# First residual sum by DMAs that add while they write

## The chip, the cores and the metric

The kernel runs on 1 core of one Trainium2 chip. The metric is the device time of one execution in microseconds; three runs of the kernel before took 1112.96, 1113.0 and 1114.12 us, median 1113.0. One further execution was profiled; all rows of views below come from it.

## The reference

One decoder layer on x of 1024 positions by 1024 channels, all in float32:

```python
h = rms_norm(x, ln_pre_mix)
proj = h @ w_in                       # pooling input, q, k, v
mix = concat(pool_out, attn_out) @ w_out
x = x + rms_norm(mix, ln_post_mix)    # the first residual sum
h = rms_norm(x, ln_pre_ffn)
f = (silu(h @ w_gate) * (h @ w_up)) @ w_down
x = x + rms_norm(f, ln_post_ffn)
```

`rms_norm(x, g)` is `x * rsqrt(mean(x*x) + 1e-6) * g`. The change concerns the line of the first residual sum alone.

## The kernel before, in words

Activations stand transposed: channels on the 128 partitions in 8 row tiles (d = 0 to 7), positions along the free axis in two halves of 512 (h = 0, 1). Every matmul is made from float32 operands that are split into a high and a low part (`hi`, `lo`), three passes each, so weights and activations are split by ScalarE (ACT: the copy that rounds to `hi`) and by VectorE or GpSimd (DVE, POOL: the subtraction that leaves `lo`). TensorE (PE) works through one fixed list of matmuls; the other engines serve it.

The stretch of the change, in order of PE's list:

* `out_proj(1, ...)`: the output projection of half 1, one row tile d after the other, 24 matmuls of 512 columns each. Its weights are loaded by SP, split by L302 (ACT) and L306 (DVE). Meanwhile `chain(0, ...)` finishes half 0: row means on PE, the power -0.5 on POOL (L332), the scale spread over partitions by four PE transposes (L261), then `add(d)`.
* `firsts(j, ...)`, j = 0 to 5: gate and up projection of half 0, 48 matmuls each, 12 for each of two banks (n = 0), then 12 more into the same two banks (n = 1). Between the two, `taken(0, i)` copies a bank to SBUF on ACT (L1453, `q<-ps_...`), and the matmuls of n = 1 into that bank can start only when the copy has read it. Meanwhile `chain(1, ...)` finishes half 1, and the block sums T1 to T4 (L1499, L1502, split by L1508 and L1509) are made from the rows of both halves.
* from there on `seven(...)`: the products of the block sums, with raw weights that `fetch` loads (L1583) and `block_sums` combines (L1548 to L1554).

In `add(d)` of the kernel before, z(d) holds the row tile of the mix. L1364 multiplies it by the gain and the scale (DVE, in place, the scale read from PSUM). L1365 adds x to it (DVE). `load` (L1360) has brought x as two transfers of 1 MB for each half, into tiles `xr`. L1369 stores the sum to DRAM from SP's queue. Then come the readers of the row: L1374 and L1375 split it (`parts`, blocks b), L1327 or L1330 square it for the next norm (`whole`), L1383 or L1493 scale it in place, L1499 and L1502 take differences.

Every engine takes its instructions in the order of its own list; an instruction that waits holds up all behind it. SP's list holds nearly all DMA issues, so a store that waits for its row holds up the loads behind it. The order of all lists except PE's comes from a scheduler that runs when the kernel is built, from start positions written in the table `PRM` (`at[...]` in `chain`).

Of the kernel before, what the change touches and what calls it, by code (L numbers as in the profile page):

```python
# [8 lines left out]
F32 = mybir.dt.float32  # L9
F32R = mybir.dt.float32r  # L10
AF = mybir.ActivationFunctionType
ALU = mybir.AluOpType
# [3 lines left out]
P = 128  # L16
# [236 lines left out]
def hybrid_block(ctx: ExitStack, tc: tile.TileContext, xT, w_in, w_v, w_vp, w_pool, w_out, w_gate, w_up, w_down,  # L253
                 g1, g2, g3, g4, pscale, cost, sint, maskA, maskB, maskD, quadA, quadB, lsel, ident, perm, band, out):
    nc = tc.nc
# [85 lines left out]
    def slot(k, shape, dt, name):  # L341

        return xgp.tile(shape, dt, name=name, tag="xk%d" % k)
# [13 lines left out]
    sq = qkp.tile([P, T], F32, name="sq", tag="vT", bufs=1)  # L357
# [176 lines left out]
    def did(key):  # L534
        seen[key] = seen.get(key, 0) + 1

    def need(key, n):
        assert seen.get(key, 0) >= n, (key, n, seen.get(key, 0))
# [724 lines left out]
    def zrows(h):  # L1263
        zs = []

        def z(d):
            if not zs:
                zs.extend(slot(2 * h + i, [P, 4, 512], F32, "z%d%d" % (h, i)) for i in range(2))
            return zs[d // 4][:, d % 4]
        return z  # L1270

    z = zrows(0), zrows(1)
# [10 lines left out]
    late = {}  # L1283
# [67 lines left out]
    def chain(h, sq, s3, at):  # L1351

        sl = slice(h * 512, (h + 1) * 512)
        x = []

        def load():
            for n in range(2):
                x.append(slot((6, 4)[h] + n, [P, 4, 512], F32, "xr%d" % n))
                with tc.issue_after(behind.ins) if h else ExitStack():
                    nc.sync.dma_start(x[n], xT[:, 4 * n:4 * n + 4, sl])  # L1360

        def add(d):
            zd = z[h](d)
            nc.vector.scalar_tensor_tensor(zd, zd, g2s[:, d:d + 1], sq.rb, op0=ALU.mult, op1=ALU.mult)  # L1364
            late["z"] = nc.vector.tensor_tensor(zd, zd, x[d // 4][:, d % 4], ALU.add)  # L1365
            did(("row", h, d))
            if h == 0:
                parts(d)
            nc.sync.dma_start(x1d[d, :, sl], zd)  # L1369

        def parts(d):
            need(("row", h, d), 1)
            zd, (hi, lo) = z[h](d), (t[:, d % 4] for t in block(d // 4, h))
            nc.scalar.activation(hi, zd, AF.Copy, scale=g3s[:, d:d + 1])  # L1374
            nc.vector.scalar_tensor_tensor(lo, zd, g3s[:, d:d + 1], hi.bitcast(F32), op0=ALU.mult, op1=ALU.subtract)  # L1375
            did(("parts", h, d))

        def whole(d):
            need(("row", h, d), 1)
            did(("whole", h, d))  # L1380
            s3.add(d, z[h](d))
            if h == 0:
                nc.scalar.activation(z[h](d), z[h](d), AF.Copy, scale=g3s[:, d:d + 1])  # L1383
                did(("scaled", d))
        return [([load], -1, 0), ([sq.mean], at[0], 0), ([sq.rows], at[1], 0),
                ([lambda d=d: add(d) for d in range(NK)], at[2], at[3]),
                ([lambda d=d: whole(d) for d in range(NK)], at[4], at[5]),
                *([([lambda d=d: parts(d) for d in range(4, NK)], at[8], at[9])] if h else []),
                ([s3.mean], at[6], 0), ([lambda: (s3.rows(r3[:, sl]), did(("r3", h)))], at[7], 0)]
# [17 lines left out]
    def block(kh, h):  # L1407

        if (kh, h) not in B:
            n = {(0, 0): 0, (1, 0): 2, (1, 1): 4}[kh, h]  # L1410
            B[kh, h] = [big(n + i, [P, 4, 512], F32R, "b%d%d" % (kh, h)) for i in range(2)]
        return B[kh, h]

    st, weights = out_proj(1, 3, sqs[1][0].add)
    weights(3)
    *chain0, mean0, rows0 = chain(0, *sqs[0], G["c0"])
    emit((st, 0.0, 1.0), *chain0, mean0)
    behind = loads[-2]
# [239 lines left out]
    def second():  # L1658
        behind_of(behind, ahead[1])
    two, again, fetch, weights = seven(0, ("P6", "P5", "P7", "P4", "P3"), nc.vector if G["fe"][EARLY] else nc.gpsimd)  # L1660
    part = 8 / len(before[0]) / EARLY
    emit(([x for f in before for x in f], 0.0, 1.0), (two[0], 1.0, 1.0 + part), (two[1], 1.0 + part, 1.0 + 2 * part),
         *chain(1, *sqs[1], G["c1"]), rows0,
         ([second], G["c3"][4], 0),
         *(([lambda a=a: behind_of(powers[-1], a)], at, 0) for a, at in zip(ahead[2:], G["ca"])), ([again], G["c3"][3], 0),
# [333 lines left out]
```

## Time and profile before

| | |
|---|---|
| median of 3 runs | 1113.0 us |
| profiled execution | 1112.79 us |
| its span, first to last instruction | 1111.0 us |
| granted TensorE clock | 0.999 |
| DMA, mean rate over the span | 182 GB/s |
| queues that DMAs are issued from | SP (200.00 MB), ACT (0.79 MB), instruction fetch |

In a row of the timeline the columns are: start, duration over all merged instructions, engine, line, operation, output<-inputs, shape, count; in brackets how long the engine sat idle before it and what released it. POOL issues no DMA in the kernel before.

### The profile page before, as it was taken

What the parts mean: (1) busy time and instruction counts of PE and PEld (TensorE: products, weight loads), DVE (VectorE), ACT (ScalarE), POOL (GpSimd) and SP (SyncE); (2) the same over time, 40 slices, a digit from 0 to 9 for tenths busy, and PEclk for the clock granted to TensorE, in tenths of its full rate; (3) what the DMA queues carried; (4) which work ended last, traced back from release to release, by engine and by line L of the source; (5) the groups of instructions that cost most, each with busy time, mean ns of one, the idle gap of its engine ahead of it and who ended that gap; (6) DMA issues with size and microseconds to landing.
All of it is one profiled execution on the core that took longest, in us unless ns stands there. A gap on an engine that the chain in (4) does not pass through costs nothing.

```text
span 1111.0 us, 16122 instructions
## 1 busy us (share of the span) xinstructions
PE 1094.3 (98%) x5694; PEld 932.5 (84%) x5694; DVE 780.3 (70%) x1340; ACT 549.4 (49%) x980; POOL 541.0 (49%) x439
## 2 busy tenths in 40 slices
PE   9999999999999999999999999999999999999997
PEld 7888999898888888888887888888888888888896
DVE  7967878787877667799777777667566462343684
ACT  7456767666677755965322222233222544343442
POOL 0111716272645021201666777686568996666521
PEclk9999999999999999999999999999999999999999
DMA  8225232424149338564466666543445895656442
GB/s 296 94 77 186 96 133 75 154 90 157 66 144 347 132 133 309 215 244 155 159 239 233 241 237 227 208 171 119 156 174 213 282 359 193 205 180 203 133 152 76
DMA packets 91296, 201.82 MB, mean 182 GB/s; under 512 B 9296, under 2 KB 25168, under 8 KB 89808
## 3 DMA queue, kind: packets, MB, share of 16 engines
q1 hardware_dynamic: 90240, 200.00, 50.6%
q8 instruction: 45, 0.74, 0.3%
q10 hardware_dynamic: 976, 0.79, 0.2%
q14 instruction: 35, 0.29, 0.1%
HBM read 143.87 MB, written 56.89 MB: 181 GB/s over the span
## 4 chain that ended last, share of the span: by engine, by line
PE 89%; DVE 4%; ACT 3%; DMA 1%; POOL 1%; issue 1%; ACTq 0%; DVEq 0%; POOLq 0%
PE ps_pj L258 28%; PE ps_s L258 25%; PE ps_o L258 24%; PE ps_t L258 10%; PE ps_t L261 2%; DMA bd<-sq 1%; ACT pp L784 1%; POOL pp L869 1%; DMA wraw<-in_w_in_dram 0%; ACT ptr L920 0%; DVE ptr L921 0%; DVE rsw L495 0%; DVE qh L526 0%; PE ps_o L261 0%; DVE ps_o L965 0%
## 5 line engine op out<-in xcount | busy, mean ns | idle before, releaser
L258 PE MATMUL ps_o<-tT,fw 128*128 128x512 f32 x648 | 150.7, 389 | 0.9 <-DVE sq L1619 0.9
L258 PEld LDWEIGHTS ps_o<-tT,fw 128*128 128x128 f32 x648 | 121.4, 188 | 26.6 <-issue 1.5
L1436 POOL TENSOR_TENSOR fw<-rw,fw 128x512 fp32r<-128x512 f32 x74 | 103.2, 1418 | 68.5 <-ACT fw L1434 67.1
L258 PE MATMUL ps_pj<-x,whl 128*128 128x512 f32 x480 | 132.7, 400 | 0.0
L258 PEld LDWEIGHTS ps_pj<-x,whl 128*128 128x128 f32 x480 | 85.7, 188 | 13.0
L306 POOL TENSOR_TENSOR whl<-wraw,whl 128x512 fp32r<-128x512 f32 x42 | 55.9, 1353 | 71.4 <-ACT whl L302 65.7
L1731 POOL TENSOR_TENSOR op<-rw,op 128x512 fp32r<-128x512 f32 x38 | 62.3, 1639 | 31.5 <-ACT op L1730 31.0
L1436 POOL TENSOR_TENSOR whl<-rw,whl 128x512 fp32r<-128x512 f32 x32 | 51.2, 1620 | 45.3 <-ACT whl L1434 34.1
L258 PE MATMUL ps_s<-b,fw 128*128 128x512 f32 x312 | 72.5, 389 | 0.0
L258 PEld LDWEIGHTS ps_s<-b,fw 128*128 128x128 f32 x312 | 58.6, 188 | 12.2
L921 DVE TENSOR_TENSOR ptr<-ps_t,ptr 128x512 fp32r<-128x512 f32 (+1 forms) x84 | 53.5, 647 | 20.4 <-ACT ptr L920 19.8
L1730 ACT ACTIVATE op<-rw 128x1024 fp32r<-128x1024 f32 x38 | 40.0, 1059 | 55.8 <-PE ps_t L258 26.5
L1434 ACT ACTIVATE fw<-rw 128x1024 fp32r<-128x1024 f32 x45 | 47.5, 1061 | 39.3 <-PE ps_o L258 15.5
L258 PE MATMUL ps_pj<-whl,x 128*128 128x256 f32 (+1 forms) x432 | 64.8, 297 | 0.0
L920 ACT ACTIVATE ptr<-ps_t 128x512 fp32r<-128x512 f32 (+1 forms) x84 | 45.7, 560 | 31.3 <-PE ps_t L261 16.2
L258 PEld LDWEIGHTS ps_pj<-whl,x 128*128 128x128 f32 x432 | 57.5, 190 | 2.4
L869 POOL TENSOR_SCALAR pp<-pp,wv 128x256 f32<-128x256 f32 x61 | 33.0, 564 | 50.9 <-DVE wv L835 49.7
L1732 DVE TENSOR_TENSOR op<-rw,op 128x512 fp32r<-128x512 f32 x33 | 28.6, 865 | 40.9 <-ACT op L1730 34.7
L332 POOL TENSOR_TENSOR nrr<-nrr,half 128x4 f32<-128x4 f32 (+1 forms) x7 | 7.4, 1054 | 96.6 <-ACT eps L331 57.4
L1731 POOL TENSOR_TENSOR fw<-rw,fw 128x512 fp32r<-128x512 f32 x26 | 42.7, 1642 | 22.4 <-ACT fw L1730 20.4
L258 PE MATMUL ps_o<-ptr,v 128*128 128x128 f32 (+3 forms) x376 | 51.1, 269 | 2.4 <-DVE ptr L921 2.3
L784 ACT ACTIVATE pp<-pp,sx 128x256 f32<-128x256 f32 x96 | 47.8, 501 | 9.9 <-DVE sx L781 9.5
(336 smaller groups left out, 2808.2 us busy)
## 6 DMA issues: line engine op xcount, KB each, us to landing
rw<-bd SPq DMA_DIRECT2D x77, 256.0 KB, 4.0
rw<-in_w_gate_dram SPq DMA_DIRECT2D x28, 512.0 KB, 4.7
rw<-in_w_up_dram SPq DMA_DIRECT2D x28, 512.0 KB, 5.7
v<-vd SPq DMA_DIRECT2D x22, 512.0 KB, 4.7
rw<-wsd SPq DMA_DIRECT2D x44, 256.0 KB, 3.8
bd<-p SPq DMA_DIRECT2D x39, 256.0 KB, 2.5
rw<-in_w_down_dram SPq DMA_DIRECT2D x33, 256.0 KB, 3.9
wraw<-in_w_out_dram SPq DMA_DIRECT2D x15, 512.0 KB, 5.1
```

The lines of the kernel that those rows point to most:

```text
L258: return tc.keep_in_program_order(nc.tensor.matmul(*a, **k))
L261: return tc.keep_in_program_order(nc.tensor.transpose(dst, src, by))
L306: pin(eng.tensor_tensor(dst[:, 1, at:at + w], src[:, at:at + w], dst[:, 0, at:at + w].bitcast(F32), ALU.subtract))
L784: nc.scalar.activation(pt[:, j, lo:], pt[:, j, lo:], AF.Exp, bias=sx[:, 0, side, j, hd, 0:1], scale=-1.0, accum_out=sx[:, 0, side, j, hd, ...
L869: nc.gpsimd.tensor_scalar(pv, pv, un.wv[:, side, j, hd:hd + 1], 1.0, op0=ALU.mult, op1=ALU.mult)
L920: nc.scalar.activation(ptr[:, 0, :w], t[:, :w], AF.Copy)
L921: nc.vector.tensor_tensor(ptr[:, 1, :w], t[:, :w], ptr[:, 0, :w].bitcast(F32), ALU.subtract)
L1434: nc.scalar.activation(dst[:, :, 0], src, AF.Copy)
L1436: low[0] = eng.tensor_tensor(dst[:, i, 1], src[:, i], dst[:, i, 0].bitcast(F32), ALU.subtract)
L1730: nc.scalar.activation(w[:, :, 0], raw, AF.Copy)
L1731: nc.gpsimd.tensor_tensor(w[:, 0, 1], raw[:, 0], w[:, 0, 0].bitcast(F32), ALU.subtract)
L1732: (nc.gpsimd if p == "P1" else nc.vector).tensor_tensor(w[:, 1, 1], raw[:, 1], w[:, 1, 0].bitcast(F32), ALU.subtract)
```

## The change

The loads of x into `xr` and the 16 additions on DVE go. In their place, behind each scaling, POOL issues a DMA that reads the same 256 KB of x from DRAM and adds them to z(d) in SBUF. `late["z"]`, behind which `fetch` is placed, is now the last such DMA.

```diff
     def chain(h, sq, s3, at):
 
         sl = slice(h * 512, (h + 1) * 512)
-        x = []
-
-        def load():
-            for n in range(2):
-                x.append(slot((6, 4)[h] + n, [P, 4, 512], F32, "xr%d" % n))
-                with tc.issue_after(behind.ins) if h else ExitStack():
-                    nc.sync.dma_start(x[n], xT[:, 4 * n:4 * n + 4, sl])
-
         def add(d):
             zd = z[h](d)
             nc.vector.scalar_tensor_tensor(zd, zd, g2s[:, d:d + 1], sq.rb, op0=ALU.mult, op1=ALU.mult)
-            late["z"] = nc.vector.tensor_tensor(zd, zd, x[d // 4][:, d % 4], ALU.add)
+            late["z"] = nc.gpsimd.dma_start(zd, xT[:, d, sl], accum_op=ALU.add)
             did(("row", h, d))
             if h == 0:
                 parts(d)
...
-        return [([load], -1, 0), ([sq.mean], at[0], 0), ([sq.rows], at[1], 0),
+        return [([sq.mean], at[0], 0), ([sq.rows], at[1], 0),
```

PE's list is the same in both kernels. Those of the other engines differ from the first scaled row to the start of the products of the block sums, some 100 us on in the trace before. In the changed kernel all lines behind 1353 have numbers lower by 8: L1364 becomes L1356, the DMA that adds is L1357, L1374 becomes L1366, L1453 becomes L1445. Three places follow.

POOL, from the last weight split ahead of the first norm of the mix to the splits of the first gate and up weights (nrr: the row scales; rw: raw gate and up weights; whl, fw: their split tiles). Before:

```order
L306 TENSOR_TENSOR whl<-wraw,whl 128x512 x4
L332 TENSOR_TENSOR nrr<-nrr,half 128x4 x2
L1436 TENSOR_TENSOR whl<-rw,whl 128x512 x2
L332 TENSOR_TENSOR nrr<-nrr,half 128x4
L1436 TENSOR_TENSOR fw<-rw,fw 128x512 x4
L332 TENSOR_TENSOR nrr<-nrr,half 128x4
```

Now:

```order
L306 TENSOR_TENSOR whl<-wraw,whl 128x512 x4
L332 TENSOR_TENSOR nrr<-nrr,half 128x4
L1357 DMA z_4187<-in_xT_dram 128x512 x4
L1357 DMA z_4188<-in_xT_dram 128x512 x4
L332 TENSOR_TENSOR nrr<-nrr,half 128x4
L1428 TENSOR_TENSOR whl<-rw,whl 128x512 x2
L332 TENSOR_TENSOR nrr<-nrr,half 128x4
L1428 TENSOR_TENSOR fw<-rw,fw 128x512 x2
L1357 DMA z_4833<-in_xT_dram 128x512 x4
L1357 DMA z_4834<-in_xT_dram 128x512 x4
L1428 TENSOR_TENSOR fw<-rw,fw 128x512 x2
```

Eight DMAs stand between the first and the second L332, and eight between two pairs of weight splits; nothing else on POOL has moved.

ACT in the output projection of half 1, up to the split of the weights of its row tile 6 (z_4187 and z_4188: rows 0 to 3 and 4 to 7 of half 0). Now:

```order
L1366 ACTIVATE b_4869<-z_4188,g3s 128x512
L1252 ACTIVATE z_4833<-ps_s 128x512
L1366 ACTIVATE b_4869<-z_4188,g3s 128x512
L1330 ACTIVATE p<-z_4187 128x512
L1375 ACTIVATE z_4187<-z_4187,g3s 128x512
L1330 ACTIVATE p<-ps_s 128x512
L1375 ACTIVATE z_4187<-z_4187,g3s 128x512
L1252 ACTIVATE z_4834<-ps_pj 128x512
L302 ACTIVATE whl<-wraw 128x1024
```

Before, between the last L1374 and the same L302:

```order
L1374 ACTIVATE b_4873<-z_4188,g3s 128x512 x4
L1252 ACTIVATE z_4837<-ps_s 128x512
L1383 ACTIVATE z_4187<-z_4187,g3s 128x512 x2
L1330 ACTIVATE p<-ps_pj 128x512
L1330 ACTIVATE p<-z_4187 128x512
L1252 ACTIVATE z_4838<-ps_pj 128x512
L302 ACTIVATE whl<-wraw 128x1024
```

The readers of the rows are spread out among the copies; between the split of row 7 and this L302 stand five instructions now and six before.

ACT in the gate and up products, from the copies of j = 1 (`q<-ps_t`) to the first copy of j = 2 (`q<-ps_s`). Before:

```order
L1453 ACTIVATE q<-ps_t 128x512
L1374 ACTIVATE b_5431<-z_4838,g3s 128x512 x4
L1330 ACTIVATE p<-z_4837 128x512
L1493 ACTIVATE z_4837<-z_4837,g3s 128x512
L1508 ACTIVATE tT_5409<-z_4187 128x512 x2
L1493 ACTIVATE z_4837<-z_4837,g3s 128x512
L1508 ACTIVATE tT_5409<-z_4187 128x512 x2
L1453 ACTIVATE q<-ps_s 128x512
```

Now (ahead of these rows, behind the copy `q<-ps_t`, stand two L1500 and one L1330):

```order
L1500 ACTIVATE tT_5401<-z_4187 128x512
L1366 ACTIVATE b_5423<-z_4834,g3s 128x512
L1500 ACTIVATE tT_5401<-z_4187 128x512
L1485 ACTIVATE z_4833<-z_4833,g3s 128x512
L1426 ACTIVATE whl<-rw 128x2x512
L1366 ACTIVATE b_5423<-z_4834,g3s 128x512
L1450 ACTIVATE p<-p 128x512
L1485 ACTIVATE z_4833<-z_4833,g3s 128x512
L1500 ACTIVATE tT_5340<-whl 128x512
L1330 ACTIVATE p<-z_4833 128x512
L1366 ACTIVATE b_5423<-z_4834,g3s 128x512
L1445 ACTIVATE q<-ps_s 128x512
```

Between the two copies stood 11 instructions; now there are 14, among them a weight split (L1426, L1434 before) and an activation (L1450, L1458 before) that stood behind the copy. On DVE, the instructions behind the eighth scaling of half 1 are now L1452, L1540, L1491, L1541, three L1491, L1501, L1542 and L1449 (before: L1460, L1548, L1499, L1549, L1499, L1509, L1550, L1457); before, the additions, L1499 and the splits L1375 stood there, and L1549 and L1550 came later.

## The prediction

> **What bounds the kernel now.** First the head of the page, then the windows of the stretch in which the lists differ, then PE's waits.
>
> ```profile
> span 1111.0 us, 16122 instructions
> PE 1094.3 (98%) x5694; PEld 932.5 (84%) x5694; DVE 780.3 (70%) x1340; ACT 549.4 (49%) x980; POOL 541.0 (49%) x439
> ```
>
> ```profile
> 416.60:472.20 55.60, 55.60 (x263) 46.21 (x262) 41.99 (x57) 40.71 (x65) 10.34 (x8) 1.00 0.69 263
> 472.20:527.70 55.50, 55.50 (x248) 46.00 (x247) 52.88 (x79) 32.14 (x51) 5.34 (x4) 1.00 0.53 199
> ```
>
> ```profile
> PE ps_s L258 <- DVE ex L812: 2.7, 2, 1.5
> ...
> PE ps_pj L261 <- POOL nrr L332: 1.0, 1, 1.0
> PE ps_o L258 <- DVE sq L1619: 0.9, 1, 0.9
> ```
>
> The windows (columns: length; busy time of PE, PEld, DVE, ACT, POOL; clock; DMA share; GB/s) show PE busy in every microsecond of 416.6 to 527.7, at full clock. PE's list isn't touched. So nothing can be won in the stretch of the change; the only waits behind it that it might touch are 1.0 and 0.9 us. The change can only be free, or make PE wait. The question is which instruction that PE needs comes late.
>
> **The change part by part. What goes, and costs nothing.** The additions leave DVE, the loads of 4 MB leave SP.
>
> ```profile
> L1365 DVE TENSOR_TENSOR z<-z,xr x16: 681/684/689, 432.6 to 482.9; 128x512 f32<-128x512 f32 x16
> ```
>
> 16 x 0.684 = 10.9 us of DVE, but PE never waited behind them: gain 0. The same 4 MB of x are read again by the new DMAs.
>
> **What is added on POOL.** Sixteen DMA issues stand in its list, in two places where it was idle:
>
> ```profile
> 424.29 1.03 POOL L332 TENSOR_TENSOR nrr<-nrr,half 128x4 f32<-128x4 f32 x1 [2.45 <-ACT nrr L327]
> 463.10 1.46 POOL L332 TENSOR_TENSOR nrr<-nrr,half 128x4 f32<-128x4 f32 x1 [37.78 <-ACT eps L331]
> 512.88 3.16 POOL L1436 TENSOR_TENSOR fw<-rw,fw 128x512 fp32r<-128x512 f32 x2 [38.50 <-ACT fw L1434]
> ```
>
> Behind the issues of half 0 waits L332 at 463.1, behind those of half 1 the split at 512.9. The first can be issued when the first row is scaled, at 427.36 + 0.74 = 428.1. That leaves 35 us for eight: up to 4.4 us each are hidden as far as POOL is concerned. Cost 0; above that it would be 8 us for each further microsecond.
>
> **When a row is ready.** Before, the last row of half 0 was ready at 432.63 + 4.90 = 437.5. Now row d is ready when its DMA has landed. Call l the time from the end of the first scaling to the first landing, and p the spacing of the landings. No transfer of this kind is in the trace; the nearest:
>
> ```profile
> 427.36 5.36 DVE L1364 SCALAR_TENSOR_TENSOR z<-z,g2s,ps_o 128x512 f32<-128x512 f32 x8 [3.84 <-PE ps_o L261]
> 432.63 4.90 DVE L1365 TENSOR_TENSOR z<-z,xr 128x512 f32<-128x512 f32 x8
> ...
> xr<-in_xT_dram SPq DMA_DIRECT2D x4, 1024.0 KB, 8.1
> xraw<-in_xT_dram SPq DMA_DIRECT2D x4, 256.0 KB, 4.2
> ```
>
> The same tensor in 256 KB lands 4.2 us after its issue, in 1 MB after 8.1, so (8.1 - 4.2) / 3 = 1.3 us for each further 256 KB. An addition must also fetch the old row: between 1.3 us (that hides) and 2.6 (it counts in full). So p is an estimate between 1.3 and 2.6, and I take 2.0, the middle, since the transfers of half 0 share the engines with eight row stores and the weight loads. For l: 4.2 with nothing added; 4.2 + 1.3 for the old row, and 1.0 more (the 1.03 us of POOL's L332, its shortest work here) for an issue by an engine that has issued none so far: 6.5. I take 5.2, the middle.
>
> **Half 0: the weights of row tile 6.** ACT's list puts the split of row 7 five instructions ahead of L302, which makes the `hi` weights that PE needs at 450.54; L306 makes `lo` from it.
>
> ```profile
> 438.70 0.40 SPq L298 DMA_DIRECT2D wraw<-in_w_out_dram  x1
> 439.65 5.60 PE L258 MATMUL ps_pj<-fw,whl 128*128 128x512 f32 x24
> 446.49 1.08 ACT L302 ACTIVATE whl<-wraw 128x1024 fp32r<-128x1024 f32 x1
> 447.43 0.74 ACT L1383 ACTIVATE z<-z,g3s 128x512 f32<-128x512 f32 x1
> 447.60 1.23 DVE L306 TENSOR_TENSOR whl<-wraw,whl 128x1024 fp32r<-128x1024 f32 x1
> 450.54 5.60 PE L258 MATMUL ps_pj<-fw,whl 128*128 128x512 f32 x24
> 450.73 0.60 ACT L1252 ACTIVATE z<-ps_s 128x512 f32<-128x512 f32 x1 [0.42 <-PE ps_s L258]
> ...
> wraw<-in_w_out_dram SPq DMA_DIRECT2D x15, 512.0 KB, 5.1
> ```
>
> The third matmul is the first to need `lo`: 450.54 + 2 x 0.23 = 451.0. Back from there: L306 1.3 with the hand-over, L302 1.0, then L1252, two L1383, two L1330 and the split itself, six of 0.6 to 0.74, in sequence some 0.1 shorter each: 3.6. Row 7 must have landed by 451.0 - 5.9 = 445.1. It lands at 428.1 + l + 7p, so PE waits for l + 7p - 17.0 where that is positive: at 5.2 and 2.0 it is **2.2 us**; at 4.2 and 1.3 nothing; at 6.5 and 2.6 it is 7.7. Row 1 stands four ACT instructions ahead of the weights of row tile 4 in the same way; it is wanted at 439.65 + 0.45 - 1.3 - 1.0 - 2.2 = 435.6, 7.5 behind 428.1, and l + p is 7.2: 0, and where it is more, PE waits earlier for a part of the same delay. The stores of the rows, L1369, now wait in SP's list for each landing, with the load of these weights behind that of row 4 (before: at 438.70, just behind all eight stores); row 4 lands at 428.1 + 5.2 + 8 = 441.3, its load 5.1 us behind the issue, two ahead of what L302 needs: 0.
>
> **Half 1: the copies of the banks.** In the gate and up products PE may go on in a bank only when ACT has copied it (L1453), and it has a slack of one bank's 12 matmuls for that.
>
> ```profile
> 472.81 5.35 DVE L1364 SCALAR_TENSOR_TENSOR z<-z,g2s,ps_o 128x512 f32<-128x512 f32 x8
> 474.78 0.43 SPq L1583 DMA_DIRECT2D rw<-in_w_up_dram  x1
> 479.88 0.68 DVE L1460 TENSOR_TENSOR p<-p,ps_pj 128x512 f32<-128x512 f32 x1
> 480.86 0.60 ACT L1453 ACTIVATE q<-ps_t 128x512 f32<-128x512 f32 x1 [1.44 <-PE ps_t L258]
> 481.80 2.57 ACT L1374 ACTIVATE b<-z,g3s 128x512 fp32r<-128x512 f32 x4 [0.34 <-DVE z L1365]
> 483.49 1.41 DVE L1499 SCALAR_TENSOR_TENSOR z<-z,g3s,z 128x512 f32<-128x512 f32 x2
> 484.81 1.22 DVE L1548 TENSOR_TENSOR wraw<-rw 128x1024 f32<-128x1024 f32 x1
> 485.15 0.71 ACT L1493 ACTIVATE z<-z,g3s 128x512 f32<-128x512 f32 x1
> 485.76 1.14 ACT L1508 ACTIVATE tT<-z 128x512 fp32r<-128x512 f32 x2
> 486.06 11.04 PE L258 MATMUL ps_s<-b,fw 128*128 128x512 f32 x48
> 488.97 0.60 ACT L1453 ACTIVATE q<-ps_s 128x512 f32<-128x512 f32 x1 [0.42 <-PE ps_s L258]
> 489.47 0.62 ACT L1458 ACTIVATE p<-p 128x512 f32<-128x512 f32 x1
> 492.19 1.05 ACT L1434 ACTIVATE fw<-rw 128x1024 fp32r<-128x1024 f32 x1
> 493.11 1.22 DVE L1549 TENSOR_TENSOR rw<-rw 128x1024 f32<-128x1024 f32 x1
> 493.66 0.62 ACT L1330 ACTIVATE p<-z 128x512 f32<-128x512 f32 x1
> ...
> rw<-in_w_up_dram SPq DMA_DIRECT2D x28, 512.0 KB, 5.7
> ```
>
> 48 matmuls in 11.04 us are 0.227 each, so the bank filled first at 488.8 is wanted back at 486.06 + 24 x 0.227 = 491.5. Before, the copy at 488.97 left 1.9 us of slack. Now 14 instructions stand between the copies of `ps_t` and this one, and they follow DVE's new list. DVE ends its scalings at 472.81 + 5.35 = 478.2 and L1460 at 478.8; then L1548, which has come forward, needs the raw weights issued at 474.78, there at about 474.78 + 5.7 = 480.5. It ends at 481.7, one L1499 at 482.4, L1549 at 483.6, the next L1499 at 484.3. Here ACT can start the second L1508. From it to the copy ACT has four L1508, two L1330, three L1374, two L1493, L1434 and L1458: at the spacing that four L1374 show (2.57 for four of 0.72: 0.1 under the duration) 2.1 + 1.0 + 1.9 + 1.2 + 1.0 + 0.5 = 7.7. The copy starts at 492.0 and ends at 492.6: PE waits **1.1 us**. Bounds: with the raw weights a microsecond earlier 0.1; with ACT's full durations (9.0) 2.4. The rows can lengthen this: the first L1374, of row 4, comes behind two L1508 and one L1330, at 484.3 + 1.6 = 485.9, and row 4 lands at 472.81 + 0.74 + l + 4p. What l + 4p has above 12.4 comes on top: **0.8 us** at 5.2 and 2.0, nothing at 4.2 and 1.3, 4.5 at 6.5 and 2.6. (Row 6, split just ahead of the copy, would need l + 6p above 17.8 beyond that; it is 17.2.) The same kind of deadline returns with the copies of j = 3, 10.9 us on; I have not priced it, the 2.4 has room for it.
>
> The delays add up, since all later work hangs on PE: 2.2 + 1.1 + 0.8 = 4.1 us. The profiled execution took 1112.79, 1.8 above its span, and the median of the runs is 1113.0; so the span becomes 1115.1 and the median **1117.1 us**. From the bounds: 1113.0 to 1113.0 + 7.7 + 2.4 + 4.5 = 1127.6.
>
> The Trainium skill, page "DMA: Bandwidth & Descriptors", section "Anatomy of one DMA — SWDGE (gpsimd) path", fits a transfer issued from GpSimd as 2.0 us plus bytes over 436 GB/s, which makes 2.6 us for 256 KB; by it l would be 2.6, no row would be late, and the sum 1.1 us, the first rival's time. The trace disagrees so far: its plain load of that size took 4.2. The same page ("Rules for kernel authors") says that an accumulating DMA reads its destination and writes it later; no run here shows that yet, and by it p would lie nearer 2.6 than 1.3.
>
> **The rivals.** *The rows land in time.* Up to p = (17.0 - 5.2) / 7 = 1.7 the split of row 7 holds up nothing, and if the raw weights land by 479.5 the copy is in time as well: not slower, 1113.0, or 1114.1 with the copy late. For it: 1.3 us for each further 256 KB, and 4 MB of `xr` less traffic ahead of it. Against: the old row has to be fetched too. *Adding is slow.* If the transfer works off a row in 4 us (about a plain load's whole 4.2), half 0 costs 5.2 + 28 - 17.0 = 16.2 and half 1 costs 5.2 + 24 - 17.8 = 11.4 by row 6: with the copy 28.7, 1141.7 us. For it: each DMA reads two places and writes one; against: nothing plain in this trace is that slow. *POOL's issue is slow.* With 5 us per DMA its 35 us of cover are gone, and p is 5: 5.2 + 35 - 17.0 + 5.2 + 30 - 17.8 = 40.6, 1153.6. *Faster.* DVE, freed of 10.9 us, would have to remove both waits of 1.0 and 0.9: 1111.1. Against: one is a POOL power behind PE's sums, not DVE's load. That the additions did not leave DVE is excluded by its list.
>
> **How the numbers follow.** About 0.2% (2.2 us) is what a measurement can tell from no change. The forecast, p from 1.7 to 2.6, has 0.52, of which 0.05 stays within 2.2 us; rows in time 0.20 (0.18 within, 0.02 slower); slow adding 0.21; slow issue 0.03; faster 0.04. So slower 0.47 + 0.02 + 0.21 + 0.03 = 0.73, same 0.23, faster 0.04. The range from 1112.5 to 1128.0 takes in the bounds and leaves out the faster case, slow issue and half of slow adding, 0.18.
>
> **What would show it.** Right: PE waits for the weights `whl` (ACT L302, DVE L306) near 450.5, about 2 us, and for ACT's `q` near 491.5, about 2 us; landings of the POOL DMAs about 5 us behind the scaling and 2 us apart; L1365 gone from DVE and POOL still idle ahead of 463. Wrong: landings 1.3 us apart and PE busy throughout (rows in time), or long waits of DVE L1375 and ACT L1374 for `z` (slow adding). A wait of PE anywhere else would mean that I followed the wrong instruction.

## The result, and the profile after

| | before | changed |
|---|---|---|
| median of 4 runs, side by side | 1112.98 us | 1124.38 us |
| lowest to highest | 1111.34 to 1114.12 | 1123.42 to 1125.44 |
| profiled execution, its span | 1112.79, 1111.0 | 1124.76, 1122.8 |
| granted TensorE clock | 0.999 | 0.993 |

The changed kernel is slower, ratio 1.0103 with a 95% interval of 1.0089 to 1.0117. The profiled span grew by 11.8 us; 4.1 had been forecast. First the head of the page and the row of the queue that POOL feeds, which is new, then PE's waits in the order of their size, then the two windows shown of before.

```profile
span 1122.8 us, 16139 instructions
PE 1099.6 (98%) x5694; PEld 935.5 (83%) x5694; DVE 773.2 (69%) x1324; ACT 549.5 (49%) x980; POOL 552.9 (49%) x455
q0 software_dynamic: 2304, 4.20, 2.1%
```

```profile
PE ps_s L258 <- ACT q L1445: 4.6, 1, 4.6
...
PE ps_pj L258 <- ACT whl L302: 1.7, 1, 1.7
...
PE ps_pj L261 <- POOL nrr L332: 1.0, 1, 1.0
PE ps_pj L258 <- DVE whl L306: 0.8, 2, 0.5
```

```profile
416.60:472.20 55.60, 53.04 (x236) 43.02 (x235) 36.45 (x49) 39.13 (x62) 15.16 (x14) 0.97 0.68 207
472.20:527.70 55.50, 50.88 (x221) 41.58 (x220) 42.98 (x62) 29.91 (x49) 14.49 (x14) 0.94 0.73 215
```

PE, busy all through these windows before, now has gaps in both, and the clock, 1.00 before, is 0.97 and 0.94. The two waits are those that the prediction named: for the weights `whl`, at the matmul that started at 450.5 before, and for ACT's copy `q`, at the one that started at 491.5. In this trace they begin at 451.6 and 497.1. The timeline shows them, with ACT's instructions that end them:

```profile
452.25 1.06 ACT L302 ACTIVATE whl<-wraw 128x1024 fp32r<-128x1024 f32 x1
453.36 0.73 PE L258 MATMUL ps_pj<-fw,whl 128*128 128x512 f32 x2 [1.74 <-ACT whl L302]
454.62 6.89 PE L258 MATMUL ps_pj<-fw,whl 128*128 128x512 f32 x22 [0.53 <-DVE whl L306]
...
501.05 0.57 ACT L1445 ACTIVATE q<-ps_s 128x512 f32<-128x512 f32 x1
501.68 7.91 PE L258 MATMUL ps_s<-b,fw 128*128 128x512 f32 x24 [4.62 <-ACT q L1445]
```

The waits are 2.3 and 4.6 us. But the 22 matmuls behind the first take 6.89 us where 22 x 0.227 are 5.0, and the 24 behind the second 7.91 where others take 5.60: the clock. The next view has the stretches of 3.41 us in which the trace shows a clock of 0.50 here, each with its neighbours (columns as in the prediction's windows).

```profile
451.78:455.19 3.41, 1.30 (x4) 0.78 (x5) 2.06 (x4) 3.39 (x5) 0.00 (x0) 1.00 1.02 411
455.19:458.61 3.42, 3.42 (x10) 2.64 (x9) 3.08 (x5) 3.20 (x6) 0.00 (x0) 0.50 0.37 81
458.61:462.02 3.41, 3.41 (x16) 2.81 (x15) 2.92 (x4) 3.35 (x7) 0.00 (x0) 1.00 0.71 288
496.16:499.57 3.41, 0.90 (x4) 0.40 (x3) 3.41 (x7) 3.30 (x6) 0.00 (x0) 1.00 1.09 263
499.57:502.98 3.41, 1.30 (x3) 1.11 (x4) 3.41 (x5) 3.41 (x7) 0.00 (x0) 0.50 1.05 396
502.98:506.40 3.42, 3.42 (x9) 2.65 (x9) 3.42 (x7) 2.34 (x4) 0.00 (x0) 0.50 0.94 358
```

A stretch in which PE was busy for 1.30 us or less is followed by one at half clock. Half of 3.42 is 1.7 us lost behind the first wait; behind the second, half of 1.30 + 3.42, 2.4 us.

How late each matmul of PE's list is against the same matmul of before gives the sum (from the starts in both traces): 0.3 us at 427; 3.6 when the third matmul of row tile 6 starts; 5.4 behind the first half clock; 10.2 when the second wait ends; 12.5 behind the second half clock; 11.4 beyond 602, where before had its wait of 0.9 for L1619 and the changed kernel has none; 12 to 13 in the last 10 us, where the clock falls in both. So the waits and their small change are some 8 us, half clock 4.0 (1.7 and 2.3), and 1.1 came back.

### The profile page after: what moved, and what is told of

It reads as the page before. It is cut to its first block, busy times and chain, and to the rows that moved or that the text cites. A ratio compares the mean times of both kernels' runs of the same rounds, so it can differ in the third digit from the quotient of the medians.

```text
span 1122.8 us, 16139 instructions
## 1 busy us (share of the span) xinstructions
PE 1099.6 (98%) x5694; PEld 935.5 (83%) x5694; DVE 773.2 (69%) x1324; ACT 549.5 (49%) x980; POOL 552.9 (49%) x455
## 4 chain that ended last, share of the span: by engine, by line
PE 84%; ACT 5%; DVE 4%; DMA 4%; issue 2%; POOL 1%; ACTq 0%; POOLq 0%
PE ps_pj L258 25%; PE ps_o L258 25%; PE ps_s L258 23%; PE ps_t L258 9%; PE ps_t L261 2%; DMA x1d<-z 2%; DMA z<-in_xT_dram 1%; ACT pp L784 1%; POOL pp L869 1%; DMA v<-vd 1%; DVE ptr L921 1%; ACT whl L302 1%; ACT ptr L920 1%; DMA wraw<-in_w_in_dram 0%; DVE rsw L495 0%
## 5 line engine op out<-in xcount | busy, mean ns | idle before, releaser
L258 PE MATMUL ps_s<-b,fw 128*128 128x512 f32 x312 | 75.0, 398 | 4.6 <-ACT q L1445 4.6
L1426 ACT ACTIVATE fw<-rw 128x1024 fp32r<-128x1024 f32 x45 | 47.5, 1060 | 44.5 <-PE ps_o L258 14.2
L332 POOL TENSOR_TENSOR nrr<-nrr,half 128x4 f32<-128x4 f32 (+1 forms) x7 | 6.7, 954 | 92.8 <-ACT eps L331 53.2
```

The source lines that it names most:

```text
L258: return tc.keep_in_program_order(nc.tensor.matmul(*a, **k))
L1426: nc.scalar.activation(dst[:, :, 0], src, AF.Copy)
```

## The experiments

Times are medians, beside runs of the kernel before on the same chip; landings of transfers are read from the semaphore events in the traces. Of longer edits the diffs show the lines that matter; `...` marks what is left out.

**One half at a time.** `e1_half0` and `e2_half1` make one half's additions by DMA and leave the other half to loads and VectorE. `e1_half0` against the kernel before (in `e2_half1` the condition is `h == 1`):

```diff
-            late["z"] = nc.vector.tensor_tensor(zd, zd, x[d // 4][:, d % 4], ALU.add)
+            if h == 0:
+                late["z"] = nc.gpsimd.dma_start(zd, xT[:, d, sl], accum_op=ALU.add)
+            else:
+                late["z"] = nc.vector.tensor_tensor(zd, zd, x[d // 4][:, d % 4], ALU.add)
...
```

> Half 0 by the DMAs that add, half 1 by loads and VectorE as before. Theory (rows of half 0 land 4.75 us behind the scaling and 2.2 apart, PE waits for the weights of row tile 6, the clock halves behind that wait): PE waits of about 3 us near 450.5 and nothing near 491.5; half clock for 3.4 us behind the wait costs 1.7 more; the rest of the program as before or up to 1 us shorter by the norm sum that is no longer waited for: 1117 to 1118. The lists of ACT are new here as well: if the split of the weights of row tile 7 comes behind late rows too, up to 3 more, 1121. Rival (the time was lost in half 1 alone, or by the new lists as such): 1113 to 1114. Rival (POOL or SP is held up by the new DMAs): long idle time of POOL or SP ahead of work that PE needs, which the theory does not have.

> Half 1 by the DMAs that add, half 0 by loads and VectorE as before. Theory (rows of half 1 land 8.4 us behind the scaling, since the first of them share the engines with raw weights, and 2.0 apart; PE waits for the copy of the bank, then half clock for 6.8 us): a PE wait of 3 to 5 us near 491.5 for ACT's q, half clock behind it worth 3.4, nothing at 450.5 for rows: 1119 to 1121. A third place is possible, since ACT now splits two weight tiles of the gate and up products ahead of the last weights of the output projection: up to 2 more. Rival (the time was lost in half 0): 1113 to 1115.

Measured: 1120.49 us (ratio 1.0070, 1.0055 to 1.0085) for half 0 alone and 1123.77 (1.0100, 1.0083 to 1.0117) for half 1 alone: the first inside its range with the third place counted in, the second 0.8 above its range even with that place. Rows of PE in the timeline, first of `e1_half0`, then of `e2_half1`:

```profile
454.43 0.87 PE L258 MATMUL ps_pj<-fw,whl 128*128 128x512 f32 x2 [2.25 <-ACT whl L302]
...
464.53 5.08 PE L258 MATMUL ps_s<-fw,whl 128*128 128x512 f32 x14 [1.16 <-DVE whl L306]
```

```profile
462.38 1.02 PE L258 MATMUL ps_o<-ones,sq 128*128 128x1 f32 x8 [2.08 <-DVE sq L1331]
...
500.08 7.17 PE L258 MATMUL ps_s<-b,fw 128*128 128x512 f32 x24 [4.97 <-ACT q L1456]
```

Each half makes its own wait: 2.25 us for `whl`, 4.97 for `q`. Each also has one more place, for which its expectation had left room: the weights of row tile 7 in the first, the sum of the squares in the second. In both, ACT's new list splits two other weight tiles first. The halves can therefore not be added up; every edit of this kernel brings new lists. The rivals that put the loss in one half alone fall.

**Without adding.** `e3_plain` issues the same DMAs with all lists of the changed kernel, but they overwrite, so it leaves the mix out of the residual sum:

```diff
-            late["z"] = nc.gpsimd.dma_start(zd, xT[:, d, sl], accum_op=ALU.add)
+            late["z"] = nc.gpsimd.dma_start(zd, xT[:, d, sl])
```

> The same DMAs without the addition: z(d) is overwritten by x, so the mix is left out of the residual sum. All lists are those of the changed kernel. Theory (the spacing of 2.0 us is the price of adding, that is of the old row's fetch beside the 1.3 us of a further 256 KB): landings 1.3 to 1.5 us apart, the wait at 450.5 gone (4.75 + 7 x 1.4 = 14.6, under 17.0), the one at 491.5 down to 1 to 3 us: 1114 to 1118. Rival (the spacing is that of transfers from POOL's queue, or of the bytes, whatever they do): landings still 2.0 apart, 1124.4 as the changed kernel.

Measured: 1118.89 us (1.0053, 1.0038 to 1.0067), 0.9 above the expected range. The landings of half 1 come 1.1 us apart on average (the last four at 484.17, 485.31, 486.74, 487.84), not 2.0, and closer than expected. The wait near 450.5 is gone, as expected; the one for `q` is still 3.5 us, above the range of 1 to 3. The page's row of POOL's queue and PE's and ACT's and DVE's rows:

```profile
q0 software_dynamic: 1280, 4.20, 1.1%
...
495.80 7.34 PE L258 MATMUL ps_s<-b,fw 128*128 128x512 f32 x24 [3.51 <-ACT q L1445]
...
488.03 0.63 ACT L1330 ACTIVATE p<-z 128x512 f32<-128x512 f32 x1 [1.33 <-DMA bd<-p]
...
482.34 1.23 DVE L1540 TENSOR_TENSOR wraw<-rw 128x1024 f32<-128x1024 f32 x1 [2.94 <-DMA rw<-in_w_up_dram]
```

Two things follow. The same 4.20 MB take POOL's queue 1.1% of the engines' time without adding and 2.1% with it: adding costs a transfer about twice the time of an engine. And in half 1 most of the wait is there with the rows in time: DVE waits for raw weights to 482.3, ACT for the store of a strip (`bd<-p`) to 488.0, and the copy stands behind both.

**The clock.** `e4_fill` puts work that nobody reads into the second wait:

```diff
+            if (j, n, i, c) == (2, 1, 0, 0):
+                spare = bank("o")
+                for k in range(16):
+                    mm(spare, w[0][:, 0, 0, :P], moving("11", 0, 0), start=(k == 0), stop=(k == 15), skip_group_check=True)
```

> The changed kernel, with 16 matmuls into a bank that nobody reads put on PE's list at the place of the long wait near 501.7, ahead of the 12 matmuls that wait for ACT's copy. Theory (the clock halves because PE stood idle for 4.6 us): the 16 take 3.6 us out of the wait, about 1 us of it stays, and the half clock behind it (6.8 us, worth 3.4) goes: 1121.0. Rival (the clock fell for another reason, load or chance): the half clock stays, 1124.4. Rival (the wait is not ACT's copy): the matmuls come on top, 1128.

Measured: 1123.23 us (1.0092, 1.0077 to 1.0107), span 1120.6: 1.2 us less in the median, 2.2 in the profiled span. The timeline and the windows of its profile, the windows cut at the same grid of 3.41 us:

```profile
453.81 0.73 PE L258 MATMUL ps_pj<-fw,whl 128*128 128x512 f32 x2 [1.88 <-ACT whl L302]
...
500.98 5.73 PE L258 MATMUL ps_s<-b,fw 128*128 128x512 f32 x24 [1.47 <-ACT q L1445]
```

```profile
450.10:453.50 3.40, 1.82 (x9) 1.16 (x7) 2.04 (x3) 3.40 (x6) 0.00 (x0) 1.00 1.03 418
453.50:456.90 3.40, 2.57 (x10) 1.82 (x11) 3.12 (x5) 3.40 (x6) 0.00 (x0) 1.00 0.68 271
497.90:501.30 3.40, 1.93 (x9) 1.29 (x8) 3.40 (x5) 3.23 (x6) 0.00 (x0) 1.00 1.06 369
501.30:504.70 3.40, 3.40 (x16) 2.81 (x15) 3.40 (x7) 3.32 (x6) 0.00 (x0) 1.00 1.00 384
```

The half clock is gone behind the second wait, so it followed PE's idle time. It is gone behind the first wait too, though that one is as long as before (1.88 + 0.53): here it fell across the border of two stretches, and neither was idle enough. What a wait costs beyond itself thus depends on where it falls on a grid that the kernel does not set. The time came down by less than the expected 3.4. In the profile PE's matmuls beyond 602 are 9.1 us late instead of 11.4: the 4.0 us of half clock are gone, and 1.7 are lost elsewhere, 0.5 of them already ahead of the first added row. In the other three runs the mean granted clock was 0.996 to 0.999, where the changed kernel had 0.993 to 0.996, so half clock is not likely to be what kept their times up; what did stays open.

**The order of ACT's list in half 1.** `e5_behind_copy` keeps half 1's squares and splits behind the second copy of j = 2:

```diff
...
-            s3.add(d, z[h](d))
+            with after_copy():
+                s3.add(d, z[h](d))
...
```

> The changed kernel, with the squares and the splits of half 1's rows (L1327, L1330, L1366) put behind the second copy of j = 2 on ACT's list; all is still computed. Ahead of the first copy remain the readers of rows 0 to 4 that make the block sums. Theory (row 4's split and what is queued behind it hold the copy: 494.7 in the changed kernel's trace, copy at 501.05, PE had waited from 497.1): the copy comes about 1.5 us behind row 4's landing, near 496.3, so the wait of 4.6 us falls to 0 to 1 and the half clock behind it goes; the work put off meets the copies of j = 3, where waits of 1 to 2 us each may appear: 1119 to 1122. Rival (the order of ACT's list does not matter, the rows or the raw weights do): a wait of 4 us or more stays at the first copy, 1124.

Measured: 1121.13 us (1.0072, 1.0053 to 1.0090). PE's waits at the two copies are 1.27 and 0.65 us, and no half clock follows; the rows land no earlier than in the changed kernel (rows 0 and 4 at 487.18 and 494.70). So with the rows as late as before, the order in ACT's list decides over most of the lateness: 3.4 of the 4.6 us at the first copy, of which 0.65 came back at the second. Expected near 496.3, the first copy came at 497.65, behind the split of a weight tile (1.05 us) that the expectation had not counted.

**The raw weights.** `e6_late_weights` puts the sums of the raw weights, for which DVE waited, behind the last difference of T3:

```diff
...
-            nc.vector.tensor_tensor(s3, raw["A11"], raw["A21"], ALU.subtract)
+            with tc.issue_after(late["sum", "T3", 3].ins):
+                nc.vector.tensor_tensor(s3, raw["A11"], raw["A21"], ALU.subtract)
```

> The changed kernel, with the sums of the raw weights (L1540 to L1543 on DVE, for which DVE waited 3.2 us) put behind the last difference of T3; all is still computed. ACT's list then has seven instructions between the splits of row 4 and the copy instead of ten, and the split of row 6 just ahead of the copy, as before. Theory (late rows hold the copy): row 6 lands near 498.7, the copy follows at about 499.5, the wait is still about 3 us: 1122 to 1123.5. Rival (the raw weights in DVE's list hold it, and the rows were there anyway): the wait at the first copy falls under 1 us: 1118 to 1120.

Measured: 1122.44 us (1.0089, 1.0073 to 1.0105), the wait 3.2 us, with a new one of 0.6 at the copies of j = 1 ahead of it. ACT in its timeline, up to the copy:

```profile
495.73 0.72 ACT L1366 ACTIVATE b<-z,g3s 128x512 fp32r<-128x512 f32 x1 [0.15 <-DMA z<-in_xT_dram]
...
497.50 0.72 ACT L1485 ACTIVATE z<-z,g3s 128x512 f32<-128x512 f32 x1 [0.53 <-DMA x1d<-z]
498.13 0.61 ACT L1330 ACTIVATE p<-z 128x512 f32<-128x512 f32 x1
498.65 0.71 ACT L1366 ACTIVATE b<-z,g3s 128x512 fp32r<-128x512 f32 x1
499.26 0.57 ACT L1445 ACTIVATE q<-ps_s 128x512 f32<-128x512 f32 x1
```

With the raw weights out of the way the rows hold the copy, through row 5's landing and then a store of a row. Together with `e3_plain` this speaks for two chains of transfers in half 1 that end within 1.5 us of each other, rows and stores on one side, raw weights and the strip's store on the other. With either out of the way most of the wait stays, 3.5 and 3.2 of the 4.6 us; no run takes away both.

**What sets the spacing of 2.0.** `e7_store4` stores four rows at a time:

```diff
...
-            nc.sync.dma_start(x1d[d, :, sl], zd)
+            if d % 4 == 3:
+                nc.sync.dma_start(x1d[d - 3:d + 1, :, sl].rearrange("n p t -> p n t"), z[h].four(d))
```

> The changed kernel, with the stores of the rows to DRAM made four rows at a time (1 MB, behind the fourth row) instead of one by one, so that rows 1 to 3 of each half land while no row is stored. Theory (2.0 us is what adding takes by itself: old row and x read, one row written): the landings of half 1 stay 2.0 apart, and the time is 1124 to 1127. Rival (the store of the row before takes a share of the engines): rows 1 to 3 land 1.3 to 1.5 apart, and the time falls by 1 to 3 us.

Measured: 1124.46 us (1.0106, two runs). In half 1 rows 0 to 4 still land 2.0 apart, as the theory said; but its reason falls in half 0, where SP's queue has nothing under way:

```
e7_store4, half 0: 435.10 437.65 438.92 440.20 441.51 443.44 444.11 445.38
changed,   half 0: 433.19 436.40 437.68 439.26 442.50 444.75 446.52 448.50
changed,   half 1: 487.35 488.71 490.71 492.71 494.70 496.71 498.71 500.71
changed, landings of SP's queue in the same time: 490.69 (p1d<-q) 492.70 (bd<-p) 494.69 (x1d<-z) 496.70 (sq<-p1d)
    498.69 (x1d<-z), and when the last row is there: 503.15 503.79 504.46 505.08 (x1d<-z, four rows)
```

A row that is added alone takes 1.28 us (437.65 to 440.20 in two steps); the step ahead of these, 2.55, has nothing of SP's queue in it either and stays unexplained. A plain 256 KB alone takes 0.64 (stores, 503.15 to 505.08 in three steps; rows that `e3_plain` loads land 0.63 and 0.66 apart at 435.11, 435.74 and 436.40). While both queues hold work the engines serve them in turn, one transfer of each in 2.0 us; 1.28 + 0.64 = 1.92. So the adding DMAs do not only come late themselves: everything that SP issues meanwhile lands at one in 2.0 us instead of one in 0.64.

**One DMA for four rows.** `e8_four_rows`:

```diff
...
-            late["z"] = nc.gpsimd.dma_start(zd, xT[:, d, sl], accum_op=ALU.add)
+            if d % 4 < 3:
+                return
+            late["z"] = nc.gpsimd.dma_start(z[h].four(d), xT[:, d - 3:d + 1, sl], accum_op=ALU.add)
...
```

> The changed kernel with one adding DMA of 1 MB for four rows in place of four of 256 KB; readers and stores come behind the fourth row. Theory (the price goes by the bytes): the two landings of half 1 are 8.0 us apart, the first about 6 us later than row 0's landing in the changed kernel, and with rows 0 to 2 waiting for row 3 the time is 1126 to 1131. Rival (a price for each DMA, issue or completion): landings 4 to 6 us apart, and no later than row 3 landed before, 1120 to 1125.

Measured: 1142.53 us (1.0268, two runs), far above both. The landings are 12.5 us apart (440.01 and 452.57, 499.72 and 512.26). POOL's timeline:

```profile
430.33 1.47 POOL L1360 DMA_DIRECT2D z<-in_xT_dram  x1 [5.10 <-DVE z L1357]
440.27 1.31 POOL L1360 DMA_DIRECT2D z<-in_xT_dram  x1 [8.47 <-issue]
```

The second issue could be made only when the first transfer had landed, so the second pays the whole way again. PE then waits 9.3 and 13.7 us at the same two places: the place is a matter of the lists, the size one of the landings.

**The order of ACT's list in half 0.** In the changed kernel row 7 landed at 448.50, in `e5_behind_copy` at 446.37, and PE's wait was no shorter there (2.24 + 0.53). Rows of ACT in these two profiles, the changed kernel first:

```profile
441.86 0.72 ACT L1375 ACTIVATE z<-z,g3s 128x512 f32<-128x512 f32 x1 [1.18 <-DMA x1d<-z]
```

```profile
444.49 0.72 ACT L1377 ACTIVATE z<-z,g3s 128x512 f32<-128x512 f32 x1 [1.33 <-DMA x1d<-z]
```

The scaling in place must wait until the store of its row has read it. `e9_scale_late` moves these scalings:

```diff
...
-            if h == 0:
+
+        def scaled(d):
+            need(("whole", h, d), 1)
+            with tc.issue_after(splits[-1].ins):
                 nc.scalar.activation(z[h](d), z[h](d), AF.Copy, scale=g3s[:, d:d + 1])
...
```

> The changed kernel, with the scalings in place of half 0's rows (L1375) put behind the split of the last weights of the output projection on ACT's list; all is still computed. In the traces of the changed kernel and of the one with half 1's readers behind the copy, ACT waits 1.2 and 1.3 us at L1375 for the store of an early row, then never again up to the split of the weights of row tile 6; and the wait of PE is as large (2.3 and 2.8 us) where row 7 lands at 446.4 as where it lands at 448.5. Theory (L1375, waiting for a store, holds ACT's list): without the four L1375 ahead of that split it comes when row 7 has landed and four instructions are done, so of the 2.3 us near 450.5 0 to 1.0 remain, no half clock behind it, and the store is waited for nowhere: 1120 to 1122, a wait of up to 1 us near 459.6 counted in, where the sum of the squares comes later. Rival (row 7's landing alone sets it, as the prediction has it): about 0.5 us less than in the changed kernel, 1.8 near 450.5, half clock stays, 1124.

Measured: 1122.98 us (1.0088, 1.0072 to 1.0104). The wait at 450.5 is gone altogether, with its half clock:

```profile
446.25 0.73 ACT L1366 ACTIVATE b<-z,g3s 128x512 fp32r<-128x512 f32 x1 [0.26 <-DMA z<-in_xT_dram]
...
448.35 1.06 ACT L302 ACTIVATE whl<-wraw 128x1024 fp32r<-128x1024 f32 x1
...
450.70 5.60 PE L258 MATMUL ps_pj<-fw,whl 128*128 128x512 f32 x24
...
500.15 7.16 PE L258 MATMUL ps_s<-b,fw 128*128 128x512 f32 x24 [5.61 <-ACT q L1448]
```

Row 7 now is what ACT waits for, and it is early enough. The time did not come down to 1120 to 1122, since waits of 0.62 and 0.65 came up for row tile 7's weights and the squares, and PE, earlier at the copy of j = 2, waits 5.6 us there instead of 4.6: the raw weights of half 1 came no earlier (DVE could start their sum at 488.44, in the changed kernel at 487.31), and its last row only 1.2 us.

The edit takes two things out from ahead of L302, the wait of 1.2 us for the store and four scalings of some 0.6 each. By itself it does not tell the two apart. `e6_late_weights`, which has the changed kernel's list here, does so in part. Its rows of ACT, row 7 landing at 446.07:

```profile
440.56 0.72 ACT L1375 ACTIVATE z<-z,g3s 128x512 f32<-128x512 f32 x1 [1.27 <-DMA x1d<-z]
...
450.96 1.05 ACT L302 ACTIVATE whl<-wraw 128x1024 fp32r<-128x1024 f32 x1
```

From the store's wait to L302 ACT works without a break, 10.4 us here and 10.4 in the changed kernel (441.86 to 452.25), wherever row 7 lands. But row 7 was close behind: without that wait ACT could have split it at 447.7 in the changed kernel, and it landed at 448.5, so L302 would have come only 0.4 us earlier. The rest is the length of ACT's list.

**Both moves.** `e10_both` has the edits of `e5_behind_copy` and `e9_scale_late`.

> Both moves of ACT's list at once: the scalings of half 0 late, half 1's squares and splits behind the second copy of j = 2; all is still computed. Theory (the time was lost to order in ACT's list and to half clock behind the waits, not to adding as such): the waits at 450.5 and 491.5 are 1 us or less each, a few of 0.5 to 2 us come up at the copies of j = 3 and 4, no half clock in the middle of the program: 1116 to 1119. Rival (ACT has too little room, work put off costs what it saves): 1121, as with one of the moves. In no case below the kernel before, which had PE busy all through this stretch.

Measured: 1118.18 us (1.0047, 1.0034 to 1.0059), inside the range. No stretch of half clock is left in the middle, and PE's waits at the copies are 0.96, 1.04 and 0.82. Of the 11.4 us lost, more than half went with the order on ACT, the half clock behind the waits counted in; the version is faster than the changed kernel and still slower than the one before, in which PE had no gap to give.

## Why the prediction was right and wrong

It was right in the sign, in the two places and in the instructions that PE waits for there, and its range held the time. Its sum was 7.7 us short of the span's growth, and the range held the time only because it was wide.

* *Gain 0; POOL's issues and SP's stores cost 0.* Right for POOL: it is busy 11.9 us longer, and PE's wait for its L332 is 1.0 as before. For SP wrong: not the issues but the transfers behind them slowed down. The weights of row tile 6, which were to land 5.1 us behind their issue, took 7.2 (442.94 to 450.13). L302 starts 2.4 us ahead of the third matmul in this trace, and PE would have been ready for that one at 452.1 (446.02 + 5.60 + 0.45); so these weights alone would have made PE wait some 0.4 us, an estimate from these rows. ACT, later still, hid it.
* *p = 2.0, the old row's fetch.* Right in size (2.0 in half 1, 2.19 on average in half 0), in part by luck. The 1.3 for a plain transfer was twice the 0.64 that it takes alone, and adding doubles that 0.64 to 1.28, so the old row's fetch does not hide; the rest of the 2.0 is the turn that SP's queue takes. The prediction named this sharing as its reason to take the middle of the bounds, but left out its other half, what it does to SP's transfers.
* *l = 5.2.* 4.75 in half 0; 8.4 in half 1, where the first rows came behind raw weights.
* *Half 0, l + 7p - 17.0 = 2.2.* Measured 2.3, with 0.3 more ahead of row tile 4's `lo`. With l and p as measured the formula gives 3.1. The agreement is chance in part: the chain that was followed back from PE was complete on ACT, but every instruction of it was taken as ready. One of them, L1375, waits for a store, and from its end on ACT's own work set L302; `e5_behind_copy` and `e6_late_weights`, with row 7 over 2 us earlier, show that it was not row 7. The path that the prediction priced was second by 0.4 us.
* *Half 1, 1.1 for the list and 0.8 for the rows.* Measured 4.6. With row 4's landing as measured the formula for the rows gives 3.4, with the 1.1 it makes 4.5; that looks like a proof and is none, since `e3_plain`, with the rows in time, still waits 3.5. The term that was mis-sized is the 1.1: its raw weights were to be there 7.7 us behind the start of the scalings (480.5 for 472.8), and DVE got them after 9.1 (487.31 for 478.19), without adding after 8.9; and L1330's wait for the strip's store, 1.1 us here, was not looked for.
* *A wait costs its length.* The prediction added the waits up as they were, and so the largest missing term is 4.0 us of half clock. The waits of before, 1.5 us at most, had left no trace in the clock.
* *Rivals.* Rows in time and slow adding fell by the landings, slow issue by POOL's idle time. The faster one was right that the wait at L1619 can go, 1.1 us; why it went here, and stays in some of the experiments, was not tried.

## What to carry to other kernels

Follow a chain back to the end for each of its instructions: who else still reads the tile it overwrites, and through which queue does that reader's transfer go? A DMA that takes over an engine's work also takes turns from every other queue, so price the transfers that share the time, not only the new ones. And a sum that agrees with the measurement is a test of nothing until one of its terms has been taken away.

## What the runs showed of the hardware that was not expected

* Adding doubles the price of a transfer: 1.28 us against 0.64 for 256 KB alone, 2.1% against 1.1% of the engines' time for the same bytes. By the Trainium skill, "DMA: Bandwidth & Descriptors", section "Anatomy of one DMA — SWDGE (gpsimd) path", 256 KB from GpSimd would take 2.6 us in all, an estimate from its fit. Counted from the end of the scaling, as the prediction counted l, the first row landed after 3.6 us where it was only loaded (`e3_plain`, 428.75 to 432.32) and after 4.75 where it was added, so the traces show more in both cases.
* Two queues with work are served in turn, here one transfer of 256 KB each in 2.0 us, whatever each costs.
* POOL's queue is finite: the eighth row's issue in half 1 waited for the first landing (issue at 487.62, landing at 487.35), and of two DMAs of 1 MB the second waited for the first. Without adding, all eight were issued before the first landed (`e3_plain`: last issue at 479.24, first landing at 480.23).

```profile
479.70 6.27 POOL L1357 DMA_DIRECT2D z<-in_xT_dram  x7
487.62 0.87 POOL L1357 DMA_DIRECT2D z<-in_xT_dram  x1 [1.65 <-issue]
```

* The clock is set anew on a fixed grid of 3.41 us. In the profiles of both kernels and all ten experiments, start and tail left out, each of the 11 stretches at full clock with PE busy for at most 1.3 us was followed by half clock, of the 16 with 1.5 to 1.95 two (both with 1.8), of the 31 with 2.05 to 2.47 none. Many of these stretches are the same places of the program in several profiles. By the Trainium skill, "TensorE: Matmul & The Clock Gate", section "What's actually happening", the window is 3413 ns long and runs freely, and the trace agrees. The same page's table in "Why this matters for your kernels" allows idle gaps up to about 3 us; here gaps of 1.7 and 0.5 us within one window were enough.
